# Query pairs of a two-layer decoder trunk: accumulator banks placed by hand, weights' high parts cast by VectorE, and stored sums of the channel mixers moved

## The chip, the cores and the metric

The kernel runs on one core of one Trainium2 chip. The metric is device time in microseconds (us), the median of several executions. The core has five instruction streams that matter here: TensorE (PE: matmuls, and PEld: the loads of its weights), VectorE (DVE), ScalarE (ACT), GpSimd (POOL) and SyncE (SP, which here only issues DMAs). Each executes its own instructions in order and waits for others by semaphores. Matmul results go to PSUM, which is used here as eight banks of 128 x 512 numbers.

## The reference

The input `x` has 1024 tokens of 1024 features. Two layers follow, each a token mixer and a channel mixer, each with an RMS norm ahead of it and a residual added behind it.

```python
for i in range(DEPTH):                       # 2
    h = rmsnorm(x, norm_mixer[i])
    x = x + (short_conv_mixer(h, ...) if i % 2 == 0 else swa_sink_attention(h, ...))
    h = rmsnorm(x, norm_ffn[i])
    g, u = split(h @ ffn_w_gate_up[i])       # 2816 columns each
    x = x + (silu(g) * u) @ ffn_w_down[i]
```

The attention of layer 1 has 16 query heads and 4 key/value heads of 64, a window of 128 tokens evaluated in blocks of 128 queries, RMS norms of the queries and keys of each head, a linear distance bias and one learned sink per head in the softmax. Everything is float32.

## The kernel before, in words

**Precision.** A float32 operand is split into a high part (a cast to the format `fp32r`) and a low part (the operand less its high part). A product is three matmuls: high by high, high by low, low by high. The cast is the "high part" and the subtraction the "low part" in what follows; most of ScalarE's and VectorE's work is such splitting.

**Fewer products.** The large products work on 2 x 2 blocks of matrices with seven products instead of eight, numbered k = 0 to 6, on sums and differences of blocks. A "granule" is the weights of one such product for one pair of output tiles, 128 x 512 numbers, split into high and low part; a product with one granule is 12 matmuls of 512 columns.

**Layout.** Features lie on the 128 partitions, tokens on the free axis. The order of the stages is: short convolution, channel mixer of layer 0, attention, channel mixer of layer 1.

**Two ways of ordering.** The convolution, both channel mixers and the keys and values of the attention are written as a line of time (`Line`, line 842): `work` appends matmuls and advances the clock `line.end`, `at(t, f)` puts anything else at a time, and `run` emits all in order of time. So a shift of a time by 1 us changes where an instruction stands among its engine's others, not when it is allowed to start. The rest of the attention is written as steps (`step`, line 2228).

**A step of the attention.** There are 64 units (i, b): query tile i of two heads, block b of 128 queries. Step n does, in the order of the letters in `ORDER` (line 58): S, the scores of unit n into bank P0 (L2075, L2076); P, a piece of whatever product runs beside; T, the transposes of unit n-2 into P1 or P3 in turn (L2118); M, bias, maxima and the copy to SBUF by VectorE (L2090); E, the exponentials of unit n-1 by ScalarE (L2110); D, divisions that are due; k, things planned for the beginning of the step; P; H, the high part of the transposed exponentials by ScalarE (L2125); L, the low part by VectorE (L2131); V, the values of unit n-3 into bank P2 (L2143, L2144); O, their copy out by ScalarE (L2161) and addition by VectorE (L2162); P; K, things planned for this step. `plan(d, f)` puts f into K of the step d later, or, with half a step, into k of the step after that.

**Query pairs.** While steps 0 to 47 run, the pieces P come from `query_pairs` (line 2284), which computes query tiles 2 to 7 as three pairs u = 1, 2, 3 with seven products each, in the order k = 0, 5, 2, 6, 1, 3, 4. Each of the 21 granules is loaded by SyncE into half of a buffer (`load_granule`), split (`split_granule`, L2332 the casts on ScalarE in two halves, L2334 the low parts, on VectorE for the first three granules and on GpSimd then) and used by the matmuls of L2392. `finish` takes the sums out of the bank (L2351 to L2365). `keep_q` then plans the head norms of a query tile: squares (L1997), statistics (L1676, L1683), the spreading of the scales by GpSimd (L1788), their transposes (L1793) and multiplication (L1798), and the split into the layout of the scores (L2027 by ScalarE, L2032 by GpSimd).

**Banks.** A bank of the kind "acc" is asked for with `bank("acc")`, of which there are four; P0 to P3 are single. Each pair asks for four: one for k = 0, 2, 3, one for k = 1, one for k = 4, one for k = 5 and 6. The products of output weights that follow the pairs (`product`, L170 and L174) ask for two each.

**Channel mixers.** `channel_mixer` (line 1064) first computes units u = 0 to 3 product by product (all four units of k = 0, then of k = 1 and so on; "not direct"), then units 4 to 21 one by one ("direct"), then the down projection. In layer 1 the order is k = 0 to 6; in layer 0 (`whole`) it is 0, 1, 6, 5, 2, 3, 4. After the last product of every odd unit, four sums of hidden halves are formed on VectorE in two calls, `f` (L1443, L1444) and `g` (L1447, L1448), into the tiles X5 and X7, and stored to HBM by three DMAs of GpSimd's queue (`stores`, L1451 to L1453) for the down projection. They stand at 5.6, 9.2 and 11.0 us after the unit, or 3.0 earlier for the first four units of layer 0 (`other`). In layer 0 the operands of the seven products are formed from X by scaling with the norm (L1208), sums such as `sum_t1` (L1276) and a split (`put`: L935 or L941 high, L936 or L942 low).

Of the kernel before, what the change touches and what calls it, by code (L numbers as in the profile page):

```python
# [15 lines left out]
P = 128  # L16
# [70 lines left out]
def trunk_kernel(ctx: ExitStack, tc: tile.TileContext, xT, small, w_in, w_out, w_qk, w_q, w_v, w_o, w_gu, w_dn, out):  # L87
# [17 lines left out]
    def plain(ap):  # L105
        return ap.bitcast(F32)
# [957 lines left out]
    def channel_mixer(layer, next_stage, src_of, operands, raw_tags, extra_tags, keep_tags, slots, begin_with=(), first_w=None, line=None, lead_in=None, before=None, follow=None):  # L1064
# [227 lines left out]
        if whole:  # L1292
            t = begin2
            for p in range(4):
                at(t + 8.0 + 2.6 * p, scale, 1, 2 * p + 1)
                put(6, p, lambda p=p: X[2 * p + 1][:, hi_half], t + 8.8 + 2.6 * p, minus=True)
                at(t + 18.0 + 2.8 * p, scale, 1, 2 * p)
                at(t + 18.7 + 2.8 * p, sum_t1, p)
                put(5, p, lambda p=p: X[2 * p][:, lo_half], t + 19.4 + 2.8 * p)
                at(t + 30.5 + 2.6 * p, sum_t2, p)  # L1300
                put(2, p, lambda p=p: T2[p // 2][:, p % 2], t + 31.2 + 2.6 * p)
                at(t + 41.5 + 2.5 * p, sum_t3, p)
                put(3, p, lambda p=p: X[2 * p][:, hi_half], t + 42.2 + 2.5 * p)
                at(t + 52.0 + 2.5 * p, sum_t4, p)
                put(4, p, lambda p=p: X[2 * p + 1][:, lo_half], t + 52.7 + 2.5 * p, minus=True)
        else:
            for p in range(4):
                at(t, scale, 1, 2 * p)
                at(t + 0.6, scale, 1, 2 * p + 1)
                at(t + 1.2, sum_t1, p)  # L1310
                at(t + 1.8, sum_t2, p)
                put(2, p, lambda p=p: T2[p // 2][:, p % 2], t + 2.4)
                t += 3.2
            t = begin2 + 20.5
            for p in range(4):
                at(t, sum_t3, p)
                put(3, p, lambda p=p: X[2 * p][:, hi_half], t + 0.6)
                t += 2.2
            for p in range(4):
                put(5, p, lambda p=p: X[2 * p][:, lo_half], t - 0.8)  # L1320
                t += 0.9
            for p in range(4):
                at(t, sum_t4, p)
                put(4, p, lambda p=p: X[2 * p + 1][:, lo_half], t + 0.6, minus=True)
                t += 2.0
            for p in range(4):
                put(6, p, lambda p=p: X[2 * p + 1][:, hi_half], t - 0.8, minus=True)
                t += 1.0
# [7 lines left out]
        def unit_product(u, k, tag, direct):  # L1336
# [97 lines left out]
            if k == (4 if other else 6):  # L1434
                if u % 2:
                    dst = hidden[layer][u // 4]
                    q = u // 2 % 2
                    tt = {}

                    def f():  # L1440
                        tt["a"], tt["b"] = slot("X5", (P, 2, HALF)), slot("X7", (P, 2, HALF))
                        he = H[u - 1]
                        dve.tensor_tensor(tt["b"][:, 1], he[:, hi_half], he[:, lo_half], ALU.subtract)  # L1443
                        dve.tensor_tensor(tt["a"][:, 0], tt["b"][:, 1], H[u][:, hi_half], ALU.subtract)  # L1444

                    def g():
                        dve.tensor_tensor(tt["a"][:, 1], H[u][:, hi_half], H[u - 1][:, hi_half], ALU.subtract)  # L1447
                        dve.tensor_tensor(tt["b"][:, 0], H[u][:, lo_half], tt["a"][:, 0], ALU.add)  # L1448

                    def stores():  # L1450
                        nc.gpsimd.dma_start(dst[6, q], H[u][:, hi_half])  # L1451
                        nc.gpsimd.dma_start(dst[2:4, q].rearrange("k p c -> p k c"), tt["a"])
                        nc.gpsimd.dma_start(dst[4:6, q].rearrange("k p c -> p k c"), tt["b"])  # L1453

                    d = 3.0 if other else 0.0
                    at(t + 5.6 - d, f)
                    at(t + 9.2 - d, g)
                    at(t + 11.0 - d, stores)
# [199 lines left out]
    def attention_layer():  # L1658
# [474 lines left out]
        def values(i, b):  # L2133
            both = PT.pop((i, b))[1]
            th, tl = both[:, 0], both[:, 1]
            kbs = key_blocks(b)
            g = 2 * (i // 4) + i % 2
            ps = bank("P2")[:, 0 : 2 * P].rearrange("p (e c) -> p e c", e=2)
            for n, kb in enumerate(kbs):
                blk = b - 1 + kb  # L2140
                first, last = n == 0, n == len(kbs) - 1
                vb = v[blk // 4][:, blk % 4, g].rearrange("p l d -> p (l d)")
                pe.matmul(ps, vb, th[:, kb], start=first, stop=False)  # L2143
                pe.matmul(ps, vb, tl[:, kb], start=False, stop=last)  # L2144
# [64 lines left out]

        units = [(i, b) for i in range(NK) for b in range(NB)]  # L2210
        NU = len(units)
        pos = {"n": -LAG, "step": 0, "free": "P1", "piece": 0}
        agenda = {}

        def plan(d, f):
# [68 lines left out]
        def query_pairs():  # L2284
# [6 lines left out]
            grans = [slot("WL", (P, 2, 4 * P), F32R, bufs=2) for _ in range(2)]  # L2291
            even_raw = {}
            last_raw = {}
            banks = {}
            loads = [(k, p) for _, k in seq if k in STREAMED for p in range(NK // 2)]
            ring = [xs[2 * p][:, :, hi_half] for p in range(NK // 2)] + [spare]
            first_rooms = {}
# [29 lines left out]
                elif j == len(seq):  # L2327
                    nc.sync.dma_start(raws[:, j % 2].rearrange("p (k c) -> p k c", c=P), w_o[0][:, 0 : len(early), :])

            def split_granule(j, i):  # L2330
                g, c = grans[j % 2], slice(i * 2 * P, (i + 1) * 2 * P)
                act.copy(g[:, 0, c], raws[:, j % 2, c])  # L2332
                lo_eng = dve if j < 3 else pool
                lo_eng.tensor_tensor(g[:, 1, c], raws[:, j % 2, c], plain(g[:, 0, c]), ALU.subtract)  # L2334

            def raw_of_odd(u):
                if u + 1 < NK // 2:
# [4 lines left out]
                return last_raw[0]  # L2342

            def finish(u, k):
                ps = banks[u, {0: "a", 1: "b", 2: "a", 3: "a", 4: "d", 5: "e", 6: "e"}[k]]
                if not even_raw:
                    even_raw[0] = slot("G7")
                even = even_raw[0]
# [28 lines left out]
            def work():  # L2377
                n = 0
                for j, (u, k) in enumerate(seq):
                    plan(0, lambda j=j: split_granule(j + 1, 0))  # L2380
                    plan(0.5, lambda j=j: split_granule(j + 1, 1))
                    load_granule(j + 2)
                    name = {0: "a", 1: "b", 2: "a", 3: "a", 4: "d", 5: "e", 6: "e"}[k]
                    if (u, name) not in banks:
                        banks[u, name] = bank("acc")
                    ps, g = banks[u, name], grans[j % 2]
# [24 lines left out]
        with tc.manual_schedule(engines={E.PE, E.Activation, E.DVE, E.Pool, E.SP}):  # L2411
# [10 lines left out]
            for k in range(NK):  # L2422
                step(work)
                if k % 2:
                    pairs.load_operand(k // 2)
                if k in (5, 6):
                    pairs.split_granule(0, k - 5)
            run(work)
            pairs.load_operand(7)
            keep_q(1, acc, pairs.odd_raw)  # L2430
# [1 line left out]
            for _ in range(NB * (NK - 2)):  # L2432
# [2 lines left out]
                        split_o(i, ("A0", "XS1", "XS3", "XS5")[i], 0)  # L2435
                step(work)
            run(work)
            w = pairs.w_last

            todo = [late[0], late[1]]  # L2440
# [154 lines left out]
```

## Time and profile before

| | |
|---|---|
| median of 3 executions | 1930.83 us (1930.39 to 1931.92) |
| profiled execution, its own time | 1930.87 us |
| its span | 1928.9 us |
| granted TensorE clock | 0.999 |
| ScalarE busy over the span | 894.0 us (46%) |
| GpSimd busy over the span | 297.6 us (15%) |
| query pairs beside the attention | about 1028 to 1167 us |

The span is the time from the first instruction to the last. Busy time is the union of an engine's instructions. A row of waits reads: waiting engine, tile and line, then the engine, tile and line that ended the wait, then the total in us, the number of times and the longest. A row of groups reads: line, engine, operation, output <- inputs, shape, count, then busy us and mean ns of one, then the idle time before them and what ended it. A row of a timeline reads: start in us, length in us, engine, line, operation, with idle time just before it in brackets. A row of one line's instructions reads: line, engine, operation, count, then shortest, median and longest in ns, first and last start, shapes.

### The profile page before, as it was taken

To read this page: it belongs to the slowest core of one execution; us is meant where nothing else is said; L and a number is where in the kernel's file an instruction comes from. 1 tells how busy PE (TensorE), PEld (TensorE's weight loads), DVE (VectorE), ACT (ScalarE), POOL (GpSimd) and SP (SyncE) were. 2 spreads that over 40 slices of the span, in tenths; PEclk is the share of its full clock that TensorE was granted. 3 is DMA by queue.
4 is the path that set the end of the run, shared out by engine and by line. 5 is a ranking of instruction groups with operands and counts; after the bars stand their busy time and mean duration, and the time that the engine had idled before them with its cause. 6 is when DMAs were issued, how large, how long until landed. Compare 5 with 4: busy or idle time off the path is not lost.

```text
span 1928.9 us, 25428 instructions
## 1 busy us (share of the span) xinstructions
PE 1918.3 (99%) x9069; PEld 1600.2 (83%) x9069; DVE 1314.6 (68%) x2269; ACT 894.0 (46%) x1777; POOL 297.6 (15%) x401
## 2 busy tenths in 40 slices
PE   9999999999999999999999999999999999999999
PEld 7888888888888888888898888888888888888887
DVE  8997877975665666556775877788656665665543
ACT  5543564633333334444546887656233333344441
POOL 0001231011111100000013565310111111100000
PEclk9999999999999999999999999999999999999999
DMA  8887595377787638985345651142675576477563
GB/s 316 260 248 157 128 247 159 112 250 214 204 232 208 156 128 311 324 237 200 105 177 198 211 201 53 60 170 82 210 215 138 201 188 168 130 248 270 197 226 101
DMA packets 151262, 368.36 MB, mean 191 GB/s; under 512 B 15072, under 2 KB 26464, under 8 KB 151136
## 3 DMA queue, kind: packets, MB, share of 16 engines
q1 hardware_dynamic: 116864, 259.49, 39.0%
q0 software_dynamic: 34128, 107.23, 22.4%
q8 instruction: 71, 1.16, 0.2%
q14 instruction: 55, 0.45, 0.1%
q10 hardware_dynamic: 144, 0.03, 0.0%
HBM read 295.12 MB, written 145.23 MB: 228 GB/s over the span
## 4 chain that ended last, share of the span: by engine, by line
PE 92%; ACT 3%; DVE 3%; issue 1%; DMA 1%; POOL 0%; SPq 0%; DVEq 0%; ACTq 0%; POOLq 0%
PE acc L1002 16%; PE acc L1005 16%; PE acc L1003 16%; PE P L1002 9%; PE P L1005 9%; PE P L1003 9%; PE acc L170 4%; PE acc L174 2%; PE acc L2392 1%; PE acc L1132 1%; PE P L2118 1%; PE acc L1134 1%; PE acc L1133 1%; PE P L1793 1%; ACT G L2110 1%
## 5 line engine op out<-in xcount | busy, mean ns | idle before, releaser
L1002 PE MATMUL acc<-XS,G 128*128 128x512 f32 x926 | 360.8, 390 | 0.0
L1005 PE MATMUL acc<-XS,G 128*128 128x512 f32 x926 | 360.6, 389 | 0.0
L1003 PE MATMUL acc<-XS,G 128*128 128x512 f32 x926 | 360.6, 389 | 0.0
L1002 PE MATMUL P<-A,G 128*128 128x512 f32 x550 | 214.6, 390 | 0.3 <-DVE G L1373 0.3
L1003 PE MATMUL P<-A,G 128*128 128x512 f32 x550 | 214.2, 389 | 0.0
L1005 PE MATMUL P<-A,G 128*128 128x512 f32 x550 | 214.2, 389 | 0.0
L1005 PEld LDWEIGHTS acc<-XS,G 128*128 128x128 f32 x926 | 173.9, 188 | 36.2
L1003 PEld LDWEIGHTS acc<-XS,G 128*128 128x128 f32 x926 | 173.9, 188 | 36.0
L1002 PEld LDWEIGHTS acc<-XS,G 128*128 128x128 f32 x926 | 173.9, 188 | 35.8
L1002 PE MATMUL acc<-A,G 128*128 128x512 f32 x442 | 172.3, 390 | 0.7 <-ACT s L1411 0.7
L1003 PE MATMUL acc<-A,G 128*128 128x512 f32 x442 | 172.1, 389 | 0.0
L1005 PE MATMUL acc<-A,G 128*128 128x512 f32 x442 | 172.1, 389 | 0.0
L936 DVE TENSOR_TENSOR G<-WR,G 128x512 fp32r<-128x512 f32 (+1 forms) x216 | 144.7, 670 | 30.0 <-ACT G L935 29.0
L936 DVE TENSOR_TENSOR G<-WL,G 128x512 fp32r<-128x512 f32 x168 | 115.2, 686 | 71.0 <-ACT G L935 71.0
L935 ACT CAST G<-WR 128x512 fp32r<-128x512 f32 (+1 forms) x216 | 130.5, 605 | 65.8 <-PE acc L1005 23.7
L935 ACT CAST G<-WH 128x512 fp32r<-128x512 f32 (+1 forms) x174 | 104.7, 602 | 87.8 <-PE acc L1005 42.1
L936 DVE TENSOR_TENSOR G<-WH,G 128x512 fp32r<-128x512 f32 (+1 forms) x174 | 115.8, 666 | 19.4 <-ACT G L935 19.3
L1334 ACT ACTIVATE G<-G 128x512 f32<-128x512 f32 x88 | 55.8, 634 | 156.4 <-DVE G L1431 151.3
L1002 PEld LDWEIGHTS P<-A,G 128*128 128x128 f32 x550 | 103.3, 188 | 22.7 <-DVE G L1373 0.7
L1005 PEld LDWEIGHTS P<-A,G 128*128 128x128 f32 x550 | 103.3, 188 | 21.5
L1003 PEld LDWEIGHTS P<-A,G 128*128 128x128 f32 x550 | 103.3, 188 | 21.3
L935 ACT CAST G<-WL 128x512 fp32r<-128x512 f32 x168 | 103.4, 616 | 31.8 <-DVE WL L884 18.9
(376 smaller groups left out, 3755.6 us busy)
## 6 DMA issues: line engine op xcount, KB each, us to landing
G<-h SPq DMA_DIRECT2D x70, 512.0 KB, 5.0
s<-in_w_dn SPq DMA_DIRECT2D x32, 704.0 KB, 8.0
h<-X POOLq DMA_DIRECT2D x44, 512.0 KB, 5.2
s<-s POOLq DMA_DIRECT2D x32, 704.0 KB, 7.0
WR<-s SPq DMA_DIRECT2D x74, 256.0 KB, 3.8
WR<-in_w_gu SPq DMA_DIRECT2D x36, 512.0 KB, 5.2
WH<-in_w_gu SPq DMA_DIRECT2D x36, 512.0 KB, 4.5
XS<-q_ops SPq DMA_DIRECT2D x36, 512.0 KB, 5.0
```

The source lines that it names most:

```text
L170: pe.matmul(ps.half(h), wh, xs[:, j, c], start=first and j == 0, stop=False)
L174: pe.matmul(ps.half(h), wl, xs[:, 0, c], start=False, stop=last)
L935: lambda: act.copy(out_hi, raw),
L936: lambda: lo_eng.tensor_tensor(out_lo, raw, plain(out_hi), ALU.subtract),
L1002: pe.matmul(ps, w[:, 0, c], x[:, 0, :], start=start and e == 0, stop=False, skip_group_check=True)
L1003: pe.matmul(ps, w[:, 0, c], x[:, 1, :], start=False, stop=False, skip_group_check=True)
L1005: pe.matmul(ps, w[:, 1, c], x[:, 0, :], start=False, stop=last, skip_group_check=True)
L1132: pe.matmul(ps, hi[:, kc], xs[:, 0, c], start=k == 0, stop=False, skip_group_check=True)
L1133: pe.matmul(ps, hi[:, kc], xs[:, 1, c], start=False, stop=False, skip_group_check=True)
L1134: pe.matmul(ps, lo[:, kc], xs[:, 0, c], start=False, stop=k == n_op - 1, skip_group_check=True)
L1334: state["silu"] = act.activation(x, x, AF.Silu)
L1793: pe.transpose(pb[:, t], wide[:, t], ident)
```

## The change

Four edits. In `query_pairs`, four "acc" banks are asked for once: two alternate between the pairs for k = 0, 2, 3 and for k = 1, one serves k = 4, 5 and 6, and the fourth receives the values of odd blocks b while the pairs run (even blocks stay in P2). The high part of a granule is cast whole by VectorE in K of the step in which the product before it begins, instead of by ScalarE in two halves, in that K and in k of the step after; the low part is one subtraction too, on the same engines as before. In the channel mixer of layer 0, the scale, `sum_t1` and split of the even tiles' second half come 1.2 us later on the line. In both channel mixers the sums and stores of odd units come 3.0 us earlier for u = 1 (in layer 0 that is where they were), and 1.0 us later for the others outside the first four units of layer 0.

```diff
-                at(t + 18.0 + 2.8 * p, scale, 1, 2 * p)
-                at(t + 18.7 + 2.8 * p, sum_t1, p)
-                put(5, p, lambda p=p: X[2 * p][:, lo_half], t + 19.4 + 2.8 * p)
+                at(t + 19.2 + 2.8 * p, scale, 1, 2 * p)
+                at(t + 19.9 + 2.8 * p, sum_t1, p)
+                put(5, p, lambda p=p: X[2 * p][:, lo_half], t + 20.6 + 2.8 * p)
...
-                    d = 3.0 if other else 0.0
+                    d = 3.0 if u == 1 or other else -1.0
                     at(t + 5.6 - d, f)
                     at(t + 9.2 - d, g)
                     at(t + 11.0 - d, stores)
...
-            ps = bank("P2")[:, 0 : 2 * P].rearrange("p (e c) -> p e c", e=2)
+            ps = pos["values"] if b % 2 and pos["values"] else bank("P2")
+            ps = ps[:, 0 : 2 * P].rearrange("p (e c) -> p e c", e=2)
...
-        pos = {"n": -LAG, "step": 0, "free": "P1", "piece": 0}
+        pos = {"n": -LAG, "step": 0, "free": "P1", "piece": 0, "values": None}
...
-            banks = {}
+            four = [bank("acc") for _ in range(4)]
+            pos["values"] = four[3]
+
+            def bank_of(u, k):
+                return four[2] if k in (4, 5, 6) else four[(u + 1) % 2 if k != 1 else u % 2]
...
-            def split_granule(j, i):
-                g, c = grans[j % 2], slice(i * 2 * P, (i + 1) * 2 * P)
-                act.copy(g[:, 0, c], raws[:, j % 2, c])
+            def split_granule(j):
+                g, raw = grans[j % 2], raws[:, j % 2]
+                dve.tensor_copy(g[:, 0], raw)
                 lo_eng = dve if j < 3 else pool
-                lo_eng.tensor_tensor(g[:, 1, c], raws[:, j % 2, c], plain(g[:, 0, c]), ALU.subtract)
+                lo_eng.tensor_tensor(g[:, 1], raw, plain(g[:, 0]), ALU.subtract)
...
-                ps = banks[u, {0: "a", 1: "b", 2: "a", 3: "a", 4: "d", 5: "e", 6: "e"}[k]]
+                ps = bank_of(u, k)
...
-                    plan(0, lambda j=j: split_granule(j + 1, 0))
-                    plan(0.5, lambda j=j: split_granule(j + 1, 1))
+                    plan(0, lambda j=j: split_granule(j + 1))
                     load_granule(j + 2)
...
-                if k in (5, 6):
-                    pairs.split_granule(0, k - 5)
+                if k == 5:
+                    pairs.split_granule(0)
...
             run(work)
+            pos["values"] = None
             w = pairs.w_last
```

More of the change, by code (lines that the diff above doesn't have):

```diff
@@ L2379, in work @@
                 for j, (u, k) in enumerate(seq):
-                    plan(0, lambda j=j: split_granule(j + 1, 0))
-                    plan(0.5, lambda j=j: split_granule(j + 1, 1))
+                    plan(0, lambda j=j: split_granule(j + 1))
                     load_granule(j + 2)
[L2383 to L2386, printed above, removed]
+                    ps, g = bank_of(u, k), grans[j % 2]
                     for p in range(NK // 2):
```

## The prediction

> **What bounds the kernel now.** I read the page first, then the waits of TensorE, then the stage in which most of the edits lie by windows, by the waits of the weight load, and by the groups and timelines of the engines that feed it.
>
> ```profile
> span 1928.9 us, 25428 instructions
> PE 1918.3 (99%) x9069; PEld 1600.2 (83%) x9069; DVE 1314.6 (68%) x2269; ACT 894.0 (46%) x1777; POOL 297.6 (15%) x401
> ```
>
> The span is TensorE from end to end: no edit here removes a matmul, so the change is worth only the time in which TensorE stands still. The waits of TensorE say where that is.
>
> ```profile
> PE P L1793 <- DVE G L2131: 1.2, 2, 0.6
> PE acc L1002 <- ACT s L1411: 0.7, 1, 0.7
> PE P L1002 <- DVE G L1373: 0.3, 1, 0.3
> ```
>
> L1793 belongs to the query pairs; L1002 to the two channel mixers, one stop in each. These idle times are too small. A 512-column matmul is recorded as about 0.39 us but the next starts 0.227 later, so a stop costs about 0.16 more than the idle shown. In the query pairs I therefore take the weight load, whose records hardly overlap (0.19 long, so about 0.04 of each 0.227 is idle anyway). The window's columns are length, then busy us and count for PE, PEld, DVE, ACT and POOL, then clock and DMA.
>
> ```profile
> 1028.00:1167.00 139.00, 135.84 (x906) 117.75 (x905) 105.78 (x325) 117.20 (x367) 75.92 (x94) 1.00 0.60 201
> PEld P L2075 <- DVE mx L2090: 3.9, 10, 1.0
> PEld P L2143 <- DVE G L2162: 2.6, 6, 1.0
> PEld P L1793 <- DVE G L2131: 1.7, 2, 0.8
> PEld P L2143 <- DVE A L2162: 0.8, 1, 0.8
> ```
>
> That is 9.0 us in 19 stops, less 19 x 0.04: **8.2 us** of the stage's 139 could go at most. All of it waits for VectorE: scores (L2075) for the maxima of the unit before (L2090) to clear bank P0, values (L2143) for the output copy (L2162) to clear P2, row transposes (L1793) for the low parts (L2131). But VectorE itself is waiting:
>
> ```profile
> DVE G L2131 <- ACT G L2125: 21.6, 21, 2.1
> L2332 ACT CAST WL<-WR 128x256 fp32r<-128x256 f32 x42 | 16.7, 399 | 2.2 <-DMA WR<-s 1.2 <-DMA WR<-in_w_q 0.9
> ```
>
> ScalarE, busy 117 of 139 us, delivers the high parts (L2125) late, and two half casts of weights (L2332) per granule stand in its queue between the output copy and L2125, twice with a DMA to wait for as well. One such place:
>
> ```profile
> 1078.85 0.39 ACT L2332 CAST WL<-WR 128x256 fp32r<-128x256 f32 x1
> 1079.14 0.57 ACT L2125 CAST G<-P 128x512 fp32r<-128x512 f32 x1
> 1079.75 0.69 DVE L2131 TENSOR_TENSOR G<-P,G 128x512 fp32r<-128x512 f32 x1 [1.70 <-ACT G L2125]
> ```
>
> The cast starts 0.29 before L2125, which starts the moment it is free; VectorE had idled 1.70. So the halves take 0.30 each off ScalarE's queue, 0.6 us per granule.
>
> **The change, part by part.** *Casts to VectorE.* Removed: 42 casts in the window, 0.30 of queue each, 12.6 us (117 to 104.6). Added: 21 casts of 128x512 on VectorE. None is in the trace; the nearest are whole weights and a gain multiply:
>
> ```profile
> L1824 DVE CAST WH<-WR x2: 685/690/695, 982.0 to 998.8; 128x1024 fp32r<-128x1024 f32 x2
> L223 DVE TENSOR_SCALAR XS<-X,cst x3: 481/489/752, 4.0 to 8.3; 128x512 fp32r<-128x512 f32 x2, 128x1024 fp32r<-128x1024 f32 x1
> ```
>
> So between 0.35 (half of 0.69) and 0.49; I take 0.42, of which 0.35 holds the queue, as L1824 is the same operation. It cannot cost less than nothing, being added work. That is 21 x 0.35 = 7.4 us on an engine that has 139 - 105.8 = 33 idle. Where the cast stands matters more: at the end of a step, behind L2162 and ahead of the next maxima, for which the scores of the unit after wait. And VectorE can be shut out by GpSimd:
>
> ```profile
> 1025.55 5.52 POOL L2032 TENSOR_TENSOR G<-G,G 64x512 fp32r<-64x512 f32 x4 [1.75 <-ACT G L2027]
> 1030.07 1.28 DVE L2334 TENSOR_TENSOR WL<-WR,WL 128x256 fp32r<-128x256 f32 x1 [0.15 <-ACT WL L2332]
> L2334 DVE TENSOR_TENSOR WL<-WR,WL x6: 418/504/1280, 1024.7 to 1034.7; 128x256 fp32r<-128x256 f32 x6
> ```
>
> A subtraction of 0.42 took 1.28: GpSimd's run ended at 1031.07, VectorE's at 1031.35. It stood until GpSimd was done. The Trainium skill ("SBUF — State Buffer", Who interferes with whom) says a VectorE copy or cast in a two-port mode and a GpSimd instruction exclude each other for a whole instruction; the trace agrees for a subtraction with two SBUF inputs (1.28 against 0.42), and shows no cast beside GpSimd. By that rule the change pays for its casts in standing time, as I reckon below.
>
> I assume casts are shut out likewise and put one, in thought, into each of the 17 steps from the fourth granule on. In five it meets another GpSimd operation; in five, four of them the same, the scores come out late. The worked one:
>
> ```profile
> 1076.67 2.64 POOL L2032 TENSOR_TENSOR G<-G,G 64x512 fp32r<-64x512 f32 x2
> 1077.16 0.48 DVE L2090 CUSTOM_DVE_ANT_0 s<-P,cst 128x192 f32<-128x192 f32 x1
> 1077.96 0.08 DVE L2090 DVE_READ_ACCUMULATOR2_ANT mx<- 128x1 f32 x1
> 1078.38 0.19 PE L2075 MATMUL P<-A,G 128*128 128x64 f32 x1
> ```
>
> The cast would come at 1077.13, wait until the first of the two ends (1077.96), and move the maxima by 0.83 + 0.35 = 1.18, from 1078.05 to 1079.23. The scores at 1078.38 would be 0.85 late. The first (no GpSimd there) and the last of the late ones:
>
> ```profile
> 1052.07 0.08 DVE L2090 DVE_READ_ACCUMULATOR2_ANT mx<- 128x1 f32 x1
> 1052.34 0.25 PE L2075 MATMUL P<-A,G 128*128 128x192 f32 x1
> 1148.02 1.28 POOL L2272 TENSOR_TENSOR A<-G,A 128x512 fp32r<-128x512 f32 x1
> 1149.71 0.08 DVE L2090 DVE_READ_ACCUMULATOR2_ANT mx<- 128x1 f32 x1
> 1150.44 0.25 PE L2075 MATMUL P<-A,G 128*128 128x192 f32 x1
> ```
>
> 0.35 against 0.18 of slack is 0.17 late; 0.42 + 0.35 against 0.65 is 0.12. The five are 0.17, 0.85, 0.21, 0.84, 0.12: **2.2 us of new stops**. Bounds: 0, as VectorE will be earlier (next), and 13, with a GpSimd wait at every granule (rivals). Were casts not shut out, the five would come to 0.2 and the sum at the end to 1923.3.
>
> What goes: L2125 comes 0.6 us sooner in the granule's step, and VectorE idles about 1 us or more before L2131 there, so L2131, L2162 and the following maxima move 0.6 forward. The stops at L1793 (1.7 in two, 0.8 each) lose 0.6 by this; the rest is covered, since TensorE comes there 0.85 later by the new stop counted above: 1.6 gone. Of the 3.9 at L2075, ten stops of 0.4, 0.6 would cover nearly all; I take 1.7 as gone (bounds 1.0 and 3.5), because part stands behind small operations of the head norms that stay.
>
> *Two banks for the values.* Odd blocks write a second bank, so L2143 no longer waits for the L2162 just issued, but for L2131, which ends one L2162 (0.43) before, and which itself comes 0.6 sooner. Seven stops, 3.4 together, 0.49 mean: 1.0 forward covers them; 3.0 gone. Bounds 2.0 to 3.4. Nothing new on TensorE.
>
> *Three accumulators by hand.* k 4, 5 and 6 share a bank. The next pair's k = 5 now waits for L2365 of k = 4, with the 12 matmuls of k = 0 between, 2.7 us at least of TensorE against one 0.69 subtraction; k = 0 gets a bank left two products earlier. I put nothing on it; if VectorE lagged over 2 us it would cost the excess, three times.
>
> *Low parts in one piece.*
>
> ```profile
> L2334 POOL TENSOR_TENSOR WL<-WR,WL 128x256 fp32r<-128x256 f32 x38 | 27.9, 736 | 41.1 <-ACT WL L2332 34.8 <-DVE G L1798 3.4 <-PE P L2144 1.6
> ```
>
> GpSimd does one 128x512 subtraction (1.28 in the L2272 row) instead of two of 0.74, and VectorE one for the first granules. The buffer is handed back to SyncE's loads half a step sooner or at the same time. Hidden by the product before; 0.
>
> *Channel mixer 1.* The second pair's sums (L1443, tiles X5 and X7) wait for the first pair's stores of the same tiles:
>
> ```profile
> 1376.52 7.10 DMA h<-X
> 1383.71 0.69 DVE L1443 TENSOR_TENSOR X<-X 128x512 f32<-128x512 f32 x1 [6.27 <-DMA h<-X]
> 1391.33 0.19 PEld L1002 LDWEIGHTS P<-A,G 128*128 128x128 f32 x1 [0.49 <-DVE s L1380]
> ```
>
> VectorE stands 6.27 us; behind it wait the splits of weights and the copies that free banks, so TensorE stops twice: 0.66 + 0.16 = 0.82 (L1411 above), and about 0.23 here (0.49 of idle load, less what the load runs ahead). The change issues sums and three stores 3 us sooner (u = 1) and the waiting sums 1 us later (u = 3). VectorE resumes near 1381. Both stops are shorter than 2.8, so **1.0 us** goes. Price if the cover fails: 1.0 stays. The other units' sums and stores move 1 us later in GpSimd's queue, ahead of the next hidden stores; tiles X5 and X7 are reused 14 products of 12 matmuls later (38 us), and the reload of the residual at a stage's end may stand up to 1 us in SyncE's queue, with weights split 13 us ahead as cover. 0; without cover 1.0 per mixer.
>
> *Channel mixer 0.* Four scales, sums and operand splits (ScalarE and VectorE, no DMA) come 1.2 us later in the schedule.
>
> ```profile
> 341.99 0.74 DVE L1208 SCALAR_TENSOR_TENSOR X<-X,cst,P 128x512 f32<-128x512 f32 x1
> 345.35 0.74 DVE L1208 SCALAR_TENSOR_TENSOR X<-X,cst,P 128x512 f32<-128x512 f32 x1
> 346.74 0.68 DVE L1373 TENSOR_TENSOR G<-P,G 128x512 f32<-128x512 f32 x1
> ```
>
> L1373 is due at 21.8 us of the stage's schedule; the second L1208 and its sum, until now at 20.8 and 21.5, fall behind it (22.0 and 22.7). L1373 runs about 1.4 sooner and the stop, 0.27 + 0.16, goes: **0.4 us**. The operand is needed some 2 us after its last split.
>
> **Sum.** Pairs: 1.6 + 1.7 + 3.0 = 6.3 gone, 2.2 new, 4.1 net. Mixers 1.4. The profiled execution took 1930.87 us (span 1928.9 and 2.0 around it), 0.04 from the median of 1930.83. 1930.8 - 5.5 = **1925.3**.
>
> **Rivals.** *Given back:* VectorE becomes the late engine and the pairs gain nothing; only the mixers' 1.4 remain: 1929.4. For it: ScalarE is freed by 12.6 while VectorE gets 7.4 and waits; the maxima's slack is small. Against: 21.6 us of VectorE's idle is ScalarE's doing. *Slower:* every cast meets GpSimd, busy 76 of 139 us, in mid operation: half of 1.28 plus 0.42, 1.06 against 0.39, the mean of the three slacks above (0.18, 0.33, 0.65), 20 x 0.67 = 13.4; and half of the 8.2 stays. +13.4 - 4.1 - 1.4 = +7.9: 1938.7. It decides once the mean wait of a cast passes 0.44, where 20 x (0.44 + 0.42 - 0.39) - 5.5 = +3.9. This is what the skill's rule gives at worst; the placing above finds an overlap in only five of 17. *All gone:* no new stop, 8.2 + 1.4: 1921.2. *Not what it says:* the four banks are requested before the last plain product asks for its two. If they are bound at request, the first pair product waits for the copies and squares of that product:
>
> ```profile
> 1027.98 1.30 PE L2392 MATMUL acc<-XS,WL 128*128 128x512 f32 x5
> 1029.94 1.08 ACT L1997 ACTIVATE G<-acc 128x512 f32<-128x512 f32 x2
> ```
>
> 1031.0 - 1028.0 = 3.0 us: 1928.3. Against it: other tiles here are requested well before they are written.
>
> **Chances.** Forecast 0.60 (its own range 1922.5 to 1928), given back 0.20, all gone 0.10, slower 0.07, bound early 0.03. About 0.2%, 3.9 us, is what a measurement of this kernel can tell from no change: faster is below 1927.0. Of the forecast 0.50 lies there, with all gone 0.60; same 0.10 + 0.20 + 0.03 = 0.33; slower 0.07. The range 1921.6 to 1930.2 leaves out the slower case and part of all gone.
>
> **What would show it.** Right: no L2332 on ScalarE, a VectorE cast near 0.42 with a few near 1.2; the wait of L2131 for L2125 well below 21.6; none of TensorE for L2162; L1443's 6.27 near 3; L1002 gone from TensorE's waits. Wrong: waits at L2075 above 6 us (given back), casts of 1 us throughout (slower), a stop of 3 us at the first pair product (bound early).

## The result, and the profile after

The changed kernel takes 1926.27 us (median of 7 runs, 1924.88 to 1927.61) against 1931.92 us for the kernel before beside it (7 runs, 1929.90 to 1933.70): a ratio of 0.9972, 95% interval 0.9960 to 0.9984, which is 5.65 us or 0.28% faster. The prediction said 1925.3, and 5.5 us faster. The profiled execution took 1926.88 us. The mean granted clock is the same on both sides: 0.9991 over these 7 runs, 0.9989 over the 23 of the kernel before beside the first experiments.

The page of the changed kernel, span and busy time:

```profile
span 1925.1 us, 25387 instructions
PE 1917.9 (100%) x9069; PEld 1604.1 (83%) x9069; DVE 1325.6 (69%) x2288; ACT 881.6 (46%) x1733; POOL 296.1 (15%) x382
```

TensorE has the same 9069 matmuls and is busy as long as before; only idle time went, 3.8 us of span. ScalarE has 12.4 us less work (12.6 had been forecast) and VectorE 11.0 us more, some 3.5 of it time in which casts stand behind GpSimd. TensorE's waits over the whole span:

```profile
PE P L326 <- DVE s L323: 1.5, 1, 1.5
PE P L2075 <- DVE mx L2090: 1.2, 3, 0.5
PE P L1676 <- DVE G L2131: 0.2, 1, 0.2
```

L1793, L2143 and L1002 are gone, in the pairs and in both mixers; scores (L2075) waiting for the maxima have risen from 0.6 us to 1.2. (The file has grown by a few lines: the values are now L2144 and L2145, the output copy L2162, its addition L2163, the cast L2338, the low part L2340, the pairs' matmuls L2394.) The stage of the pairs by window, by the waits of the weight load and by those of VectorE:

```profile
1028.00:1167.00 139.00, 137.78 (x927) 122.09 (x927) 119.43 (x352) 107.52 (x332) 76.25 (x78) 0.99 0.61 201
```
```profile
PEld P L2075 <- DVE mx L2090: 2.4, 7, 0.7
PEld P L2075 <- issue: 1.7, 2, 0.9
```
```profile
DVE G L2131 <- ACT G L2125: 6.7, 11, 0.9
...
DVE WL L2338 <- DMA WR<-s: 2.2, 1, 2.2
DVE WL L2338 <- PE acc L174: 1.6, 1, 1.6
```

The wait of VectorE for ScalarE's high parts has fallen from 21.6 us to 6.7. The weight load's stops have fallen from 9.0 us in 19 to 4.1 in 9, all at L2075. The two put down to "issue" are of the same kind: they are the 64-column scores at 1078.0 and 1126.7 us, whose matmul is shown waiting for the maxima (two of the three of L2075 in TensorE's waits). The casts themselves, and one of the places where they hurt, on VectorE, GpSimd and the weight load:

```profile
L2338 DVE CAST WL<-WR x22: 412/428/1493, 1024.3 to 1158.9; 128x512 fp32r<-128x512 f32 x22
```
```profile
1097.35 0.43 DVE L2163 TENSOR_TENSOR G<-P,G 64x256 f32<-64x256 f32 x1
1097.70 1.49 DVE L2338 CAST WL<-WR 128x512 fp32r<-128x512 f32 x1
1099.22 0.48 DVE L2090 CUSTOM_DVE_ANT_0 G<-P,cst 128x192 f32<-128x192 f32 x1
```
```profile
1097.45 1.46 POOL L2032 TENSOR_TENSOR G<-WH,G 64x512 fp32r<-64x512 f32 x1 [0.35 <-ACT G L2027]
```
```profile
1100.16 0.19 PEld L2075 LDWEIGHTS P<-A,G 128*128 128x128 f32 x1 [0.73 <-DVE mx L2090]
```

The typical cast takes 0.43 us. This one began while GpSimd's L2032 was running, stood until that ended at 1098.91 and finished at 1099.19; the maxima behind it came a microsecond late, and TensorE stopped.

In the rest of the text, "by start-to-start" means the time from one matmul's start to the next one's, less what the same pair of lines usually takes, added up from the trace. By that measure the stage from 1028 to 1167 us lost 8.2 us before and loses 4.0 now, besides 1.5 for the halved clock:

| stops of the pairs' stage, start-to-start | before | after |
|---|---|---|
| at L1793 (row transposes) | 2.1 | 0.1 |
| at the values | 2.6 | 0.2 |
| at L2075, L2076 (scores) | 2.5 | 2.9 |
| others | 1.1 | 0.9 |

Mixer 1 went from 1.3 to 0, mixer 0 from 0.5 to 0 and the products of output weights behind the pairs from 2.4 to 1.9. That is 6.5 us of stops. Some 3 us of them do not show in the span of this one execution, as TensorE works through two stretches of halved clock in it and through none in the profile of before; 3.8 us of span and 3 us of clock make 6.8. One of these stretches also covers a stop of 1.1 us that the casts alone show (see the runs without the banks). An execution without it should therefore show less than 6.5 us gone, nearer to the 5.65 of the medians; none of the changed kernel was profiled.

### The profile page after: what moved, and what is told of

Same layout as the page of the kernel before. It is cut to its first block, busy times and chain, and to the rows that moved or that the text cites. A ratio compares the mean times of both kernels' runs of the same rounds, so it can differ in the third digit from the quotient of the medians.

```text
span 1925.1 us, 25387 instructions
## 1 busy us (share of the span) xinstructions
PE 1917.9 (100%) x9069; PEld 1604.1 (83%) x9069; DVE 1325.6 (69%) x2288; ACT 881.6 (46%) x1733; POOL 296.1 (15%) x382
## 4 chain that ended last, share of the span: by engine, by line
PE 96%; DVE 2%; ACT 1%; issue 1%; POOL 0%; POOLq 0%; DVEq 0%; ACTq 0%
PE acc L1002 16%; PE acc L1003 16%; PE acc L1005 16%; PE P L1002 10%; PE P L1003 10%; PE P L1005 10%; PE acc L170 4%; PE acc L2394 2%; PE acc L174 2%; PE P L2118 1%; PE acc L1132 1%; PE acc L1134 1%; PE acc L1133 1%; PE P L1676 1%; PE P L1793 1%; PE P L2075 1%
## 5 line engine op out<-in xcount | busy, mean ns | idle before, releaser
L1002 PE MATMUL acc<-XS,G 128*128 128x512 f32 x926 | 360.4, 389 | 0.0
L1002 PE MATMUL P<-A,G 128*128 128x512 f32 x550 | 214.1, 389 | 0.0
L1002 PEld LDWEIGHTS acc<-XS,G 128*128 128x128 f32 x926 | 173.8, 188 | 36.1
L1002 PE MATMUL acc<-A,G 128*128 128x512 f32 x442 | 172.1, 389 | 0.0
L1002 PEld LDWEIGHTS P<-A,G 128*128 128x128 f32 x550 | 103.2, 188 | 21.4
```

Of the source, the lines that this page charges most:

```text
L1002: pe.matmul(ps, w[:, 0, c], x[:, 0, :], start=start and e == 0, stop=False, skip_group_check=True)
```

## The experiments

All are compared with the kernel before, run beside them; the changed kernel's own ratio is 0.9972.

| run | median us (runs) | before, us | ratio, 95% interval |
|---|---|---|---|
| mixers' edits alone | 1930.28 (11) | 1931.85 | 0.9993, 0.9984 to 1.0002 |
| casts alone | 1926.97 (7) | 1931.85 | 0.9974, 0.9964 to 0.9985 |
| banks alone | 1932.51 (11) | 1931.85 | 1.0001, 0.9993 to 1.0010 |
| late cast | 1923.35 (5) | 1931.85 | 0.9961, 0.9948 to 0.9973 |
| change without banks | 1925.62 (7) | 1931.61 | 0.9971, 0.9960 to 0.9982 |
| late cast without banks | 1924.42 (5) | 1931.61 | 0.9962, 0.9949 to 0.9974 |
| whole cast on ScalarE | 1928.39 (11) | 1931.61 | 0.9984, 0.9975 to 0.9993 |
| late cast but for one | 1925.90 (6) | 1931.61 | 0.9969, 0.9957 to 0.9980 |
| cast twice | 1937.35 (5) | 1931.99 | 1.0032, 1.0020 to 1.0044 |
| no earlier sums | 1927.57 (1) | 1931.99 | one run |
| late cast, again | 1924.66 (5) | 1931.99 | 0.9964, 0.9951 to 0.9976 |
| late cast but for one, again | 1923.41 (5) | 1931.99 | 0.9959, 0.9946 to 0.9973 |

**The mixers alone.** The kernel before with these edits and no other:

```diff
-                at(t + 18.0 + 2.8 * p, scale, 1, 2 * p)
+                at(t + 19.2 + 2.8 * p, scale, 1, 2 * p)
...
-                    d = 3.0 if other else 0.0
+                    d = 3.0 if u == 1 or other else -1.0
```

> The kernel before with the two edits of the channel mixers alone. Theory (the edits are worth what each saves by itself): L1002 goes from TensorE's waits in both mixers, the weight load's stop at L1002 in mixer 1 too; 1.4 us faster by the prediction's steps, up to 2.1 by the start-to-start times of the changed kernel's trace; so a ratio of 0.9989 to 0.9993. The waits of the query pairs (L1793, L2143, L2075) stay as they were before. Rival (the mixers' stops lie ahead of other stops that take them back): 0 us, ratio 1.000.

Measured: 1.6 us between the medians, and an interval that includes no change. The trace has no L1002 among TensorE's waits. One row of VectorE's waits in mixer 1 (1360 to 1400 us), where 6.27 us stood before:

```profile
DVE X L1443 <- DMA h<-X: 0.3, 1, 0.3
```

So the stops of the two mixers, 1.8 us by start-to-start, are gone, and the time agrees with that without proving it. In this profile a stop of 0.6 us at L1185 near 326 us, which no other profile here has, takes part of it back.

**The casts alone.** The edit of the change in `split_granule` and its three calls, banks and mixers as before:

```diff
-                act.copy(g[:, 0, c], raws[:, j % 2, c])
+                dve.tensor_copy(g[:, 0], raw)
```

> The kernel before with the casts of the pairs' weights moved to VectorE alone, banks as before. Theory (ScalarE's queue made the high parts late; 0.6 us per granule): VectorE's wait at L2131 for L2125 falls from 21.6 us to below 10; L1793 goes from TensorE's waits (-1.6), stops at L2075 go (-1.7) and new ones come (+1.6 to +2.2), and L2143's 3.4 us shrink to below 1.5, as the values' copy also comes up to 0.6 sooner: 1.5 to 4 us faster. Rival A (the banks are what counts; L2143 waits for the addition just issued, whoever casts): L2143 keeps over 2.5 us and the change is below 1 us. Rival B (given back): L2075 rises by more than 3 us, 0 or slower.

Measured: 4.9 us faster, nearly all that the whole change brings; but the mean clock of these 7 runs was 0.9996 against 0.9989 in the kernel before, which is up to 1.3 of the 4.9. Waits of the weight load in the pairs' stage, and one row of VectorE's:

```profile
PEld P L2075 <- DVE mx L2090: 2.9, 5, 1.3
PEld P L2075 <- issue: 1.7, 2, 0.8
```
```profile
DVE G L2131 <- ACT G L2125: 6.0, 10, 0.8
```

L2143 does not appear, though P2 is the only bank for the values here. Rival A falls, and B too (3.9 has become 4.6). A surprise: mixer 1 has no stop at L1002 either, though its sums were not moved. The wait at L1443 was 4.6 us this time, not 6.3, because the stores before it landed sooner (the one that ended the wait in 5.7 us instead of 7.1): the row of these DMAs (tile h, 1366 to 1386 us), in the kernel before and here.

```profile
DMA to landing us min/median/max: 2.6/5.4/7.1
```
```profile
DMA to landing us min/median/max: 3.0/5.6/5.9
```

**The banks alone.** The change's `bank_of`, `four` and `pos["values"]`, casts on ScalarE in halves.

```diff
-            ps = bank("P2")[:, 0 : 2 * P].rearrange("p (e c) -> p e c", e=2)
+            ps = pos["values"] if b % 2 and pos["values"] else bank("P2")
...
-                ps = banks[u, {0: "a", 1: "b", 2: "a", 3: "a", 4: "d", 5: "e", 6: "e"}[k]]
+                ps = bank_of(u, k)
```

> The kernel before with the four banks (three accumulators by hand, values in two banks in turn) alone, casts on ScalarE as before. Theory: L2143 leaves the wait for the addition L2162 just issued (0.43 us) and so loses 2 to 3.4 us of its stops, L1793 (1.7) and L2075 (3.9) stay as they were: 2 to 3 us faster. Rival (TensorE only comes 0.4 us sooner to the next place that waits for VectorE): L2075 and L1793 grow by what L2143 loses, under 1 us faster. A stop at the head of a k = 4, 5 or 6 product (L2392 waiting for a subtraction L2355 to L2365) would show that the shared accumulator costs; theory: none.

Measured: no difference. Waits of the weight load in the pairs' stage:

```profile
PEld P L2075 <- DVE mx L2090: 5.2, 12, 0.8
PEld P L1793 <- DVE G L2131: 1.7, 2, 0.9
...
PEld P L2145 <- DVE G L2131: 0.2, 1, 0.2
```

The 3.4 us at L2143 are gone, and L2075 has grown from 3.9 to 5.2: TensorE gets past the values 0.4 us sooner and meets the same late VectorE at the next scores. By start-to-start the stage lost 1 to 2 us less than before, which the runs do not show. No pair product stopped behind the shared accumulator. This decides mostly for the rival: the wait moved.

**The late cast.** The changed kernel with one number changed, which puts each cast behind the next maxima instead of ahead of them:

```diff
-                    plan(0, lambda j=j: split_granule(j + 1))
+                    plan(0.5, lambda j=j: split_granule(j + 1))
```

> The changed kernel with each cast half a step later, at k of the next step: behind the maxima of that step and ahead of its low part, instead of ahead of the maxima. Theory (the cast ahead of the maxima makes the scores of the next unit late): the three stops at L2075 near 1077.2, 1099.5 and 1125.9 us (0.70, 0.58 and 0.70 with the loss around each) vanish: 2.0 us faster than the changed kernel, 7.6 faster than before, ratio 0.996. Rival (VectorE has no room there either): the same delay falls on L2131, the values or row transposes stop instead, and the time is that of the changed kernel or up to 2 us more. Casts that meet a GpSimd operation stay near 1.0 us wherever they fall on one.

Measured: 1923.35 us, 8.5 less than before. Waits of the weight load in the pairs' stage, and the casts:

```profile
PEld acc L2394 <- POOL WL L2340: 1.2, 1, 1.2
PEld P L2075 <- DVE mx L2090: 0.5, 1, 0.5
PEld P L1676 <- DVE G L2131: 0.3, 1, 0.3
```
```profile
L2338 DVE CAST WL<-WR x22: 416/421/872, 1024.2 to 1157.5; 128x512 fp32r<-128x512 f32 x22
```

The three stops near 1077, 1099 and 1126 us are gone, so by the trace the theory holds: the place ahead of the maxima was the price. One new stop has come, 1.0 us at the matmuls of granule 19 (L2394). Its low part on GpSimd, asked for half a step later, now stands behind another subtraction:

```profile
1145.72 1.28 POOL L2273 TENSOR_TENSOR A<-G,A 128x512 fp32r<-128x512 f32 x1
1146.97 1.28 POOL L2340 TENSOR_TENSOR WL<-WR,WL 128x512 fp32r<-128x512 f32 x1
```

**The change, and the late cast, without the banks.** Both again with the bank edit undone, that is the lines of the diff under the banks alone the other way round.

> The changed kernel without its bank edit (casts on VectorE and both mixers' edits stay). Theory, formed on the runs of single parts (casts alone took 4.9 us, banks alone nothing): once the casts have left ScalarE, the output copy is early enough for bank P2, so L2143 stays out of TensorE's waits and the banks are worth only the one stop of 1.2 us near 1042.7 us that casts alone still show: 1927.0 less about 1, 0.5 to 1.5 us slower than or as fast as the changed kernel, ratio near 0.997. Rival (the prediction's step: the banks are worth up to 3.0 us): 3 us slower than the changed kernel, ratio 0.9987, with L2143 back in the waits.

> The late cast (k of the next step, behind the maxima) without the bank edit. Theory: here the cast delays the low part and with it the addition L2162 by 0.35 to 0.42 in each granule's step, and with bank P2 alone the next values (L2143) wait for that addition; so the banks are worth something only here: stops at L2143 of 1 to 3 us in all, 1924.4 to 1926.4. Rival (the values never come close): no L2143 among the weight load's waits, time that of the late cast with banks, 1923.4.

Measured: 1925.62 us, as the changed kernel (1926.27), and 1924.42 us, between the two measurements of the late cast with banks (1923.35 and 1924.66). Neither trace has a stop of over 0.1 us at the values. The first run's theory is right that no 3 us hang on the banks, and wrong about the one stop of 1.2 us near 1042.7 us: it is absent here without banks, so the banks had not removed it. The traces show what did. The cast and the stop in the run of the casts alone, then the same cast in the changed kernel:

```profile
1042.71 0.43 DVE L2332 CAST WL<-WR 128x512 fp32r<-128x512 f32 x1 [1.78 <-PE P L2144]
1043.99 0.36 PE L2075 MATMUL P<-A,G 128*128 128x192 f32 x1 [0.91 <-DVE mx L2090]
```
```profile
1042.50 0.43 DVE L2338 CAST WL<-WR 128x512 fp32r<-128x512 f32 x1 [0.33 <-PE P L2076]
```

The rows name TensorE, but what the cast waits for is its weights: their load, issued at 1036.44 and 1036.60 us, landed 6.2 and 5.8 us later, and the cast starts 0.1 us behind that in both, and likewise at 1042.63 without the banks. In the changed kernel and without the banks, a stretch of halved clock near 1035 us had held TensorE back by some 1.5 us, so its scores were not due yet; in the casts alone there is no such stretch, and they stood. The stop is covered by the clock there, not removed by an edit. That the changed kernel would show it without the stretch follows from this, but no profile shows it.

In the second run my theory fell and the rival held. With the casts gone from ScalarE, the banks' edit was worth nothing that these runs can tell.

**The whole cast on ScalarE.**

```diff
-                dve.tensor_copy(g[:, 0], raw)
+                act.copy(g[:, 0], raw)
```

> The changed kernel with the high part cast whole by ScalarE instead of VectorE, at the same place. It tells the engine from the granularity. Theory (ScalarE's queue is what made L2125 late): one cast of 128x512 (0.57 to 0.62 on ScalarE) holds the queue about as long as the two halves (0.6), so VectorE's wait at L2131 for L2125 stays above 15 us, and with the banks in place the stops sit at L1793 and L2075: the time of the kernel before less the mixers' 1.2, 1929.5 to 1931.5. Rival (one piece instead of two, or the place, made the gain): the time of the changed kernel, near 1926.3.

Measured: 1928.39 us, 1.1 below the range expected, but 2 us above the changed kernel. VectorE's and the weight load's waits in the pairs' stage:

```profile
DVE G L2131 <- ACT G L2125: 20.6, 21, 2.5
```
```profile
PEld P L2075 <- DVE mx L2090: 5.0, 10, 1.1
PEld P L1793 <- DVE G L2131: 1.5, 2, 0.8
```

The wait is back where it was before (21.6), and the stops at L2075 and L1793 with it: by start-to-start the stage loses 7.3 us against the change's 4.0. By the waits, it is the engine whose queue the cast stands in that counts. By the times this is less sure: of the 2.1 us, about 1.1 are the lower mean clock of these runs (0.9985 against 0.9991), and the profiled execution, at 1930.25, was the slowest of the eleven. What one piece instead of two, and the banks, may be worth beside ScalarE's casts is at most the 1.9 us between this run and the mixers alone; it was not taken apart, so up to a third of the 5.65 us may be theirs.

**The cast done twice.**

```diff
+                for _ in range(2):
+                    dve.tensor_copy(g[:, 0], raw)
```

> The changed kernel with every cast of the pairs' weights done twice by VectorE, the second over the first; the result is the same. It prices VectorE's queue ahead of the maxima and puts the prediction's rival 'given back' to the test. Theory (the cast stands ahead of the maxima, whose slack was 0.18, 0.33 and 0.65 in three places): each granule's maxima come another 0.35 later; with a mean slack of 0.39 about half of some 20 granules stop TensorE, for 0.2 to 0.35 each, and the three long stops at L2075 grow by 0.35 each: 3 to 5 us slower than the changed kernel, 1929 to 1931.5, all of it at L2075. Rival (VectorE has room, the cast meets only GpSimd's instructions): only the casts shut out by GpSimd get longer, under 1.5 us slower.

Measured: 1937.35 us, 11 us more than the changed kernel, more than either theory gave. Waits of the weight load, then one place on VectorE, GpSimd and TensorE:

```profile
PEld P L2075 <- DVE mx L2090: 7.1, 15, 1.7
PEld P L2075 <- issue: 5.2, 2, 2.6
```
```profile
1078.88 2.77 DVE L2339 CAST WL<-WR 128x512 fp32r<-128x512 f32 x2
1081.69 0.48 DVE L2090 CUSTOM_DVE_ANT_0 s<-P,cst 128x192 f32<-128x192 f32 x1
```
```profile
1078.68 2.69 POOL L2032 TENSOR_TENSOR G<-G,G 64x512 fp32r<-64x512 f32 x2
```
```profile
1082.72 0.27 PE L2075 MATMUL P<-A,G 128*128 128x64 f32 x1 [2.20 <-DVE mx L2090]
```

Two casts beside two subtractions of GpSimd took 2.77 us instead of 0.85: the first waits out the rest of one subtraction, the second the whole of the next. That happened at 1079 and 1131 us, 2.4 us of TensorE each by start-to-start, and at 1156 us, 1.5. So most of the added stops come from GpSimd's instructions and not from the casts' own length, as in the prediction's rival "slower". The mean granted clock was also lower here (0.997 against 0.999 over the runs), which is 1930 x 0.002, about 4 of the 11 us.

**The sums of u = 1 not moved forward.** Everything else as in the change:

```diff
-                    d = 3.0 if u == 1 or other else -1.0
+                    d = 3.0 if other else -1.0
```

> The changed kernel without the 3.0 us earlier sums of u = 1 (the 1.0 us later ones of the other units stay). The casts alone had VectorE waiting 4.6 us at L1443 in mixer 1 and no stop of TensorE at L1002, the kernel before 6.3 us and two stops (0.93 and 0.34 with the loss behind them). Theory (what counts is whether the wait passes a cover of 4.6 to 6.2 us): the wait is about 5.3 (6.3 less 1.0), and TensorE stops for 0 to 0.5 us in all. Rival (the 3 us are what removed the stops): both stops stay, 1 us or more.

Measured, in one run: the weight load has no wait between 1360 and 1400 us, and VectorE waits as long as in the run of the casts alone.

```profile
DVE X L1443 <- DMA h<-X: 4.2, 1, 4.2
```

The theory's cover holds: 4.2 and 4.6 us of waiting cost TensorE nothing, 6.2 (banks alone) and 6.3 (before) cost it two stops. The 5.3 expected was too long since the stores landed in 4.3 us at most, not 7.1. That is no accident of this run: in the eleven profiles with the mixers' edits, whole or in part, the slowest store of this window took 3.9 to 4.6 us, in the three without them 5.9 to 7.1. Before, a load of weights (L1477) is issued 0.15 us ahead of one of the stores; in the changed kernel it comes 1.1 us behind the last of them, and here 1.0 us ahead of the first. That the two slow each other fits, but was not tested. So the 3 us shorten the wait further, to 0.3; whether the 1 us alone would do when the stores take 7.1 is open.

**The late cast for all granules but one, and both once more.** To remove the late cast's one stop, granule 19 keeps the place it has in the change:

```diff
-                    plan(0.5, lambda j=j: split_granule(j + 1))
+                    plan(0 if j == 18 else 0.5, lambda j=j: split_granule(j + 1))
```

> The late cast for all granules but one: granule 19's stays where the changed kernel has it, as its low part on GpSimd came behind a 1.28 us subtraction (L2273) with the late cast, and TensorE stopped 1.0 us at 1147.1 us for it (the one stop at L2394). Theory: that stop goes, at most 0.2 comes at L2075: 0.8 to 1.0 us faster than the late cast for all, about 1922.5, ratio 0.9957. Rival (the stop moves to the next place that is late): 1923.4 as before.

> The late cast once more, beside the late cast for all but granule 19 on the same chip, to see whether the latter's lower granted clock (a mean of 0.998 over six runs against 0.999 here) belongs to the kernel. Theory (the clock's short drops fall by chance): this one is at 1923 to 1925, and 0.8 to 1.8 us slower than its companion. Rival (the closer TensorE is packed, the more often the clock drops): this one keeps a mean clock of 0.999 or more and is 1 to 2 us faster than its companion.

> The late cast for all granules but granule 19, once more. Theory (the drops fall by chance): mean clock near 0.999 as in the other kernels, 1922 to 1923.5, the fastest of all. Rival (denser work draws more drops): mean clock 0.998 again and 1925 to 1926.5, although the stops in the trace are the fewest.

Measured: 1925.90 and then 1923.41 us; the late cast beside it, 1924.66. The trace does what the theory says. All that is left of the weight load's waits in the pairs' stage (second measurement):

```profile
PEld P L2075 <- DVE mx L2090: 1.1, 4, 0.5
PEld P L1676 <- DVE G L2131: 0.2, 1, 0.2
```

By start-to-start the stage loses 2.0 us, against 3.0 for the late cast and 4.0 for the change, clock aside. The times do not order them as surely: the first measurement had a mean clock of 0.998 over its runs, the second 0.999, as the late cast had in both. So the lower clock need not belong to the kernel, and over both measurements the two late versions (medians 1923.4 to 1925.9) cannot be told apart. Both beat the kernel before in every run, and by their medians the changed kernel, by 0.4 to 2.9 us; their intervals overlap the changed kernel's.

## Why the prediction was right, point by point

The theory behind it was that VectorE's lateness in the pairs was ScalarE's doing, that the casts were what made ScalarE late, and that a cast on VectorE costs only where it delays a maximum. The rivals were that the banks, or the single piece, made the gain, and that VectorE would give it back.

- **The bound.** Right: 3.8 us of span went and no matmul. At most 8.2 us were there to gain in the pairs; 4.2 were gained by start-to-start, 4.1 had been forecast. That the two are so close is partly luck: 1.1 of the 4.2 is a stop that the halved clock covers in this trace.
- **L2125 sooner, VectorE's wait well below 21.6.** Right, 6.7; shown by casts alone (6.0) against the whole cast on ScalarE (20.6).
- **L1793, 1.6 gone.** Right in kind: both stops went, 2.0 with what lies behind a stop.
- **L2075, 1.7 gone.** All of the old stops went but the last, which shrank from 0.8 to 0.2: some 2.3 us. The small operations of the head norms cost less than I allowed for.
- **The two banks, 3.0 gone at the values.** The stops went, 2.4 by start-to-start, but this is the step whose cause was wrong. I had added 0.6 from the cast and 0.43 from the bank against a mean stop of 0.49, and booked the sum under the banks. The cast's 0.6 covers it alone: without banks no stop at the values returns, and with banks alone the stop moves to L2075. The sum held because I had not counted the gain twice.
- **New stops, 2.2.** Right, 2.4, but one is missing from the forecast: the cast at 1042.5 us, which waits for its weights and costs 1.1 where TensorE comes there in time (casts alone). The five late scores were forecast at 0.17, 0.85, 0.21, 0.84 and 0.12; by start-to-start they came at 0.11, 0.70, 0.57, 0.70 and 0.10, and a sixth of 0.2. The third was underestimated: VectorE, sooner than before, reached its cast 0.25 us after GpSimd's L2032 had begun (1097.70 and 1097.45), where by the profile of before it would have come some 0.7 into it, and so stood for nearly all of it.
- **The cast at 0.42, shut out by GpSimd.** Right: 0.41 to 0.43 free, and 0.90 to 1.49 in five places, as many as forecast. The Trainium skill ("SBUF — State Buffer", Who interferes with whom) says that a VectorE cast in a two-port mode and a GpSimd instruction exclude each other for a whole instruction. There are rows for a cast now, and the traces agree, in the cast-twice run most plainly (2.77 for 0.85); no row names the mode. The rival built on it, "slower", asked for such a meeting at every granule; there were five, and the cast-twice run shows what it is like when the meetings count.
- **Shared accumulator, low parts, early binding: 0.** Right for the accumulator (no stop at L2394 from L2357 to L2371 in any run with banks) and for the early binding. The low parts in one piece on GpSimd cost nothing in the change, but they are the next to be late: the late cast's stop of 1.0 us is theirs. One wait I had not seen: granule 1's cast stands 1.6 us for its buffer, which the last plain product (L174) still reads; it stopped nothing.
- **Mixers, 1.0 and 0.4.** The stops went, 1.3 and 0.5 with what lies behind them. The wait at L1443 was forecast near 3 and was 0.3, as the stores landed in 4.3 us at most instead of 7.1. The casts alone lost the stop in mixer 1 without the edit, as their stores too landed sooner (5.7 us), so this 1.0 was partly the luck of one trace.
- **The rivals.** "Given back" fell: VectorE still waits for ScalarE. "All gone" fell by the new stops, and the late cast, which I had not thought of as a version, came within some 2 us of it.

## What to carry to other kernels

When TensorE waits for one engine and that engine waits for another, take work from the last in the chain; room made nearer to TensorE (here the banks) only moves the stop to the next place. Where the taken work is put decides how much of the gain is kept: put it behind the instruction for which TensorE waits next, not ahead of it (here one number, half a step: 2 us of stops by the trace, which the times alone do not separate). Before charging a gain to one edit, see whether another one covers the same stop alone.

## What the runs showed of the hardware

**The granted clock drops to half for some microseconds.** Two stretches of the changed kernel, with a normal one before each and after them; the columns are those of the other windows, the clock is the last but two:

```profile
1030.00:1034.50 4.50, 4.50 (x32) 4.04 (x31) 1.51 (x5) 1.02 (x3) 1.11 (x1) 1.00 0.87 304
1034.90:1037.40 2.50, 2.50 (x9) 2.10 (x8) 1.06 (x6) 1.31 (x5) 2.31 (x3) 0.50 0.93 335
1178.20:1181.40 3.20, 3.20 (x13) 2.90 (x12) 2.30 (x7) 1.94 (x8) 0.44 (x1) 0.50 0.02 5
1182.00:1186.00 4.00, 4.00 (x28) 3.51 (x26) 3.05 (x9) 2.73 (x9) 2.62 (x4) 1.00 0.00 0
```

In them 512-column matmuls start 0.427 us apart instead of 0.227. By windows set around them each lasts 3.4 us (1034.7 to 1038.2 and 1178.1 to 1181.5) and costs some 1.4 to 1.8 us by start-to-start; the first one of the cast-twice run lasts 6.8 us. The profiles of before and of the casts alone have none from 20 us to the last matmul. In the other profiles they begin at 1034 to 1035, at 1156 to 1163 or at 1174 to 1188 us, and they differ between runs of one kernel: the late cast had one of them in its first profile and two in its second. That is as much as an edit is worth here: a mean clock of 0.998 instead of 0.999 is 1.9 us. What sets them off stays open.

**VectorE and GpSimd shut each other out both ways.** The copies of L1788 on GpSimd take 0.61 us; one that began 0.07 us after a cast of VectorE took 0.825, while the cast kept its 0.43. A subtraction of L2032 that began 0.17 us into another cast took 1.41 instead of 1.29.

```profile
L1788 POOL COPY G<-hr_y x14: 612/614/825, 1022.2 to 1164.5; 128x512 f32<-128x512 f32 x14
```

In these rows whoever comes second waits, so a cast in VectorE's queue also costs GpSimd. A short overlap is free: the same cast, at 1035.57 us, had begun 0.14 us before the end of an earlier copy and lost nothing.
